# Joined 512-column matmuls of the high weights in chosen stages, an early first activation of TensorE, and 64x64 work put in groups

## The chip, the cores and the metric

The kernel runs on one core of one Trainium2 chip. What counts is the device time of one execution in microseconds (us). Before the change it is 2953.51 us, the median of 3 runs (2952.63 to 2953.68).

## The reference

The reference chains two transformer blocks over 256 tokens of width 1024 in float32; each block has two layers. What matters of them here:

```python
def swiglu(x, w_in, w_out):
    gate, up = jnp.split(x @ w_in, 2, axis=-1)
    return (jax.nn.silu(gate) * up) @ w_out

for l in range(2):                                   # first block
    h = h + 0.5 * swiglu(rms_norm(h, ffn1_norm[l]), ffn1_w_in[l], ffn1_w_out[l])
    u = rms_norm(h, mix_norm[l])
    ...                                              # u @ w_in[l]; state space branch y_s, delta rule branch y_d
    merged = sigmoid(gate_s) * (y_s @ ssm_w_branch[l]) + sigmoid(gate_d) * (y_d @ dn_w_branch[l])
    h = h + merged @ w_out[l]
    h = h + 0.5 * swiglu(rms_norm(h, ffn2_norm[l]), ffn2_w_in[l], ffn2_w_out[l])
for l in range(2):                                   # second block
    h = h + mixer_sublayer(...)                      # retention and a wide convolution, ends with @ w_mix_out
    h = h + memory_cross_attention(...)
    h = h + conv_ffn(...)                            # ends with @ w_down
```

A feed forward is 1024 to 2x2816 and 2816 back to 1024. There are four of the first block's kind (`ffn`) and two of the second's (`conv_ffn`). The delta rule needs the inverse of small triangular matrices, which the kernel makes by doubling blocks of 2 up to 64.

## The kernel before

**Numbers in two parts.** TensorE multiplies in a float32 form with a shorter mantissa (F32R). To keep precision, each operand is split into a rounded high part and a low rest. A product is three matmuls: high weights by high input, high weights by low input, low weights by high input.

**Weights.** `wpart` (L180 to L190) loads 128x1024 weights (one output tile, eight input tiles) on SyncE's DMA queue into `wr`, lets ScalarE round them into `wh` (L187), and VectorE subtract to get `wl` (L189). Each pool has four buffers, and `wpart` runs at high priority, so weights are made as far ahead as the buffers go.

**Inputs.** Activations are feature-major: a tile of 128x512 holds two feature tiles (256 tokens each). Class `X` keeps a list of high tiles and one of low tiles, each 512 wide; `h(k)` and `l(k)` cut 256 columns out of one.

**The product.** `proj_fm` (L201) makes two output tiles (m = 0, 1) of 256 columns side by side in one PSUM bank (`pw`, four of them). For each input tile k it issues three matmuls of 256 columns (L213, L214, L215), each with its own weight load. `proj_tm2` (L235) has the roles swapped: x is stationary, and the weights move in 512 columns (L246 to L248).

**The feed forward.** `ffn` (L350) runs 11 rounds j; in each a gate and an up product, `pg` and `pu`, are multiplied by `rbb` (1/rms of each token) on the way out of PSUM, since the input isn't normalised yet when the products begin; then silu, product, and the split into `hid`. `Norm.finish` gives `rb` some us after the stage has begun. `out_proj` (L345) multiplies by the second weights in four steps, each evicted by one VectorE instruction onto h (L368), which then feeds the next norm. `Norm.scaled` (L285) makes an input that is normalised, so that later products need no `rbb`; before, only the mixers use it.

**The delta rule.** `delta` (L497) is a generator that is advanced between projections (`tick`). Near its end, a loop over eight blocks alternates a 64x64 transpose (L621) and a 64x64 matmul (L622); then eight 64x64 matmuls follow (L630). It runs twice in each of the first block's layers.

**The order.** A planner simulates the program and writes the order of each engine's instructions from priorities; within an engine it is then fixed.

Of the kernel before, what the change touches and what calls it, by code (L numbers as in the profile page):

```python
# [15 lines left out]
P = 128  # L16
# [8 lines left out]
AHEAD = 100000  # L25
PUMP = 3.1
# [47 lines left out]
def _kernel(tc, t):  # L74
    nc = tc.nc
    V, A, G, TE = nc.vector, nc.scalar, nc.gpsimd, nc.tensor
    with ExitStack() as es:
# [5 lines left out]
        hp, xp = pool("hp", 4), pool("xp", 4)  # L83
# [16 lines left out]

        def pw():
            return pwp.tile([P, 512], F32, name="pw")
# [5 lines left out]
        g0 = cp.tile([P, 8], F32, name="g0")  # L108
        with tc.high_priority(offset=AHEAD):
            nc.sync.dma_start(g0, t["v1"][:, OFF1["ffn1_norm"][0]:OFF1["ffn1_norm"][0] + 8])  # L110
# [43 lines left out]
        def split(hi, lo, src):  # L154
            A.copy(hi, src)
            sub(lo, src, hi.bitcast(F32))
# [35 lines left out]
        class X:  # L192
            def __init__(self):
                self.hi, self.lo = [], []

            def h(self, k):
                return self.hi[k // 2][:, (k % 2) * 256:(k % 2) * 256 + 256]

            def l(self, k):
                return self.lo[k // 2][:, (k % 2) * 256:(k % 2) * 256 + 256]  # L200

        def proj_fm(w, i, KT, x):

            p = pw()
            for m in range(2):
                o = p[:, m * 256:m * 256 + 256]
                for k0 in range(0, KT, 8):
                    kt = min(8, KT - k0)
                    hi, lo = wpart(w[i + m, :, k0 * 128:(k0 + kt) * 128], kt * 128)
                    for kk in range(kt):  # L210
                        k = k0 + kk
                        a, b = hi[:, kk * 128:kk * 128 + 128], lo[:, kk * 128:kk * 128 + 128]
                        TE.matmul(o, a, x.h(k), start=(k == 0), stop=False)  # L213
                        TE.matmul(o, a, x.l(k), start=False, stop=False)  # L214
                        TE.matmul(o, b, x.h(k), start=False, stop=(k == KT - 1))  # L215
                    tick()
            return p

# [36 lines left out]
        class Norm:  # L255
            def __init__(self, g, alloc=None):
                self.g, self.x, self.acc = g, X(), None
                self.alloc = alloc
# [5 lines left out]
            def operand(self, j, h):  # L264
                if self.alloc is None:
                    hi = xp.tile([P, 512], F32R, name="xh")
                    lo = xp.tile([P, 512], F32R, name="xl")
                else:
                    hi, lo = self.alloc(F32R), self.alloc(F32R)
                for m in range(2):  # L270
                    k = 2 * j + m
                    s = slice(m * 256, m * 256 + 256)
                    A.activation(hi[:, s], h[:, s], AF.Copy, scale=self.g[:, k:k + 1])
                    V.scalar_tensor_tensor(lo[:, s], h[:, s], self.g[:, k:k + 1], hi[:, s].bitcast(F32), op0=ALU.mult, op1=ALU.subtract)
                self.x.hi.append(hi)
                self.x.lo.append(lo)
# [8 lines left out]
            def scaled(self, h):  # L285

                y = X()
                for j in range(4):
# [4 lines left out]
                    hi, lo = xp.tile([P, 512], F32R, name="xh"), xp.tile([P, 512], F32R, name="xl")  # L293
                    split(hi, lo, v)
                    y.hi.append(hi)
                    y.lo.append(lo)
# [48 lines left out]
        def out_proj(w, KT, x, evac):  # L345
            for j in range(4):
                evac(j, proj_fm(w, 2 * j, KT, x))


        def ffn(h, L, nrm, w1, w2, nxt):  # L350
# [3 lines left out]
            for j in range(NF // 2):  # L354
                pg = proj_fm(w1[L], 2 * j, 8, x)
                pu = proj_fm(w1[L], NF + 2 * j, 8, x)
                g, u = cv(), cv()
                mul(r2(g), r2(pg), rbb)
                A.activation(g, g, AF.Silu)
                mul(r2(u), r2(pu), rbb)  # L360
                mul(g, g, u)
                hi, lo = sa(F32R), sa(F32R)
                split(hi, lo, g)
                hid.hi.append(hi)
                hid.lo.append(lo)

            def evac(j, p):
                V.scalar_tensor_tensor(h[j], p, 0.5, h[j], op0=ALU.mult, op1=ALU.add)  # L368
                nxt.feed(j, h[j])
            out_proj(w2[L], NF, hid, evac)  # L370
# [32 lines left out]
        def to_features(tm, u, g, dst):  # L403
# [5 lines left out]
            hi, lo = sa(F32R), sa(F32R)  # L409
            n = 512 // g.shape[1]  # L410
            for m in range(g.shape[1]):
                s = slice(m * n, m * n + n)
                A.activation(hi[:, s], p[:, s], AF.Copy, scale=g[:, m:m + 1])
                V.scalar_tensor_tensor(lo[:, s], p[:, s], g[:, m:m + 1], hi[:, s].bitcast(F32), op0=ALU.mult, op1=ALU.subtract)
            dst.hi.append(hi)
            dst.lo.append(lo)

        def mixer1(h, L, nrm, nxt):
# [97 lines left out]
            def delta(hh, kf, qf, vf, zd):  # L516
# [296 lines left out]
            def evac_s(j, p):  # L813
                V.scalar_tensor_tensor(gs[j], gs[j], 1.0, p, op0=ALU.add, op1=ALU.mult)
                add(gs[j], gs[j], gd[j])
                hi, lo = sa(F32R), sa(F32R)
                split(hi, lo, gs[j])
# [517 lines left out]
```

## Time and profile before

| what | value |
|---|---|
| runs, median (lowest to highest) | 2953.51 us (2952.63 to 2953.68) |
| profiled execution, its own time | 2955.59 us |
| its span, first to last instruction | 2953.8 us |
| matmuls, and as many weight loads | 24912 |
| busy: TensorE, VectorE, ScalarE | 99%, 75%, 51% |

The span is what the rows tell of; 1.8 us of the profiled execution lie around it. In the rows PE is TensorE's matmul side, PEld its weight loads, DVE VectorE, ACT ScalarE, SPq the instruction queue of SyncE. A matmul's duration in the rows is from entry to exit of a pipeline, so durations overlap: the pace is read from start to start, or from the number in a stretch.

### The profile page before, as it was taken

To read this page: it belongs to the slowest core of one execution; us is meant where nothing else is said; L and a number is where in the kernel's file an instruction comes from. 1 tells how busy PE (TensorE), PEld (TensorE's weight loads), DVE (VectorE), ACT (ScalarE), POOL (GpSimd) and SP (SyncE) were. 2 spreads that over 40 slices of the span, in tenths; PEclk is the share of its full clock that TensorE was granted. 3 is DMA by queue.
4 is the path that set the end of the run, shared out by engine and by line. 5 is a ranking of instruction groups with operands and counts; after the bars stand their busy time and mean duration, and the time that the engine had idled before them with its cause. 6 is when DMAs were issued, how large, how long until landed. Compare 5 with 4: busy or idle time off the path is not lost.

```text
span 2953.8 us, 59625 instructions
## 1 busy us (share of the span) xinstructions
PE 2936.0 (99%) x24912; PEld 2840.5 (96%) x24912; DVE 2202.1 (75%) x3498; ACT 1516.1 (51%) x2016; POOL 98.7 (3%) x113
## 2 busy tenths in 40 slices
PE   8999999999999999999999999999999999999998
PEld 8999998999999999999999988999999988999998
DVE  6658878866566589688666799976676899876774
ACT  5446555554444465465444544545554544554553
POOL 0000001100000000011000000000000000000000
PEclk9999999999999999999999999999999999999999
DMA  6555444456565555344556555555456555554554
GB/s 230 178 183 173 151 137 142 156 182 185 178 186 180 182 175 163 126 147 150 179 182 195 170 188 167 172 175 168 157 181 194 185 173 167 172 179 150 174 181 132
DMA packets 141679, 505.34 MB, mean 171 GB/s; under 512 B 16164, under 2 KB 16550, under 8 KB 141408
## 3 DMA queue, kind: packets, MB, share of 16 engines
q1 hardware_dynamic: 137808, 490.29, 52.2%
q0 software_dynamic: 3312, 10.70, 1.3%
q8 instruction: 195, 3.19, 0.4%
q14 instruction: 76, 0.62, 0.1%
q10 hardware_dynamic: 288, 0.52, 0.0%
HBM read 500.32 MB, written 1.13 MB: 170 GB/s over the span
## 4 chain that ended last, share of the span: by engine, by line
PE 99%; DMA 0%; DVE 0%; issue 0%; ACT 0%; SPq 0%; POOLq 0%; DVEq 0%
PE pw L213 26%; PE pw L215 26%; PE pw L214 26%; PE pw L246 3%; PE pw L248 3%; PE pw L247 3%; PE pm L764 1%; PE pm L408 1%; PE pw L229 1%; PE pw L231 1%; PE pw L230 1%; PE pm L585 0%; PE pm L1080 0%; PE pm L1106 0%; PE pm L599 0%; PE pm L983 0%
## 5 line engine op out<-in xcount | busy, mean ns | idle before, releaser
L187 ACT CAST wh<-wr 128x1024 fp32r<-128x1024 f32 (+1 forms) x938 | 970.4, 1036 | 1223.9 <-PE pw L214 879.2
L189 DVE TENSOR_TENSOR wl<-wr,wh 128x1024 fp32r<-128x1024 f32 (+1 forms) x938 | 1130.2, 1207 | 521.1 <-ACT wh L187 512.0
L213 PE MATMUL pw<-xh,wh 128*128 128x256 f32 x3712 | 1066.3, 288 | 7.8 <-ACT wh L187 7.7
L214 PE MATMUL pw<-xl,wh 128*128 128x256 f32 x3712 | 1058.7, 285 | 0.0
L215 PE MATMUL pw<-xh,wl 128*128 128x256 f32 x3712 | 1056.4, 285 | 0.7 <-DVE wl L189 0.7
L214 PE MATMUL pw<-sa,wh 128*128 128x256 f32 x2656 | 752.7, 284 | 0.0
L213 PE MATMUL pw<-sa,wh 128*128 128x256 f32 x2656 | 751.8, 284 | 0.7 <-DVE sa L137 0.7
L215 PE MATMUL pw<-sa,wl 128*128 128x256 f32 x2656 | 751.6, 283 | 0.0
L213 PEld LDWEIGHTS pw<-xh,wh 128*128 128x128 f32 x3712 | 716.5, 193 | 13.3 <-ACT wh L187 10.0
L214 PEld LDWEIGHTS pw<-xl,wh 128*128 128x128 f32 x3712 | 717.2, 193 | 5.4 <-issue 4.6
L215 PEld LDWEIGHTS pw<-xh,wl 128*128 128x128 f32 x3712 | 716.7, 193 | 2.7 <-DVE wl L189 1.3
L214 PEld LDWEIGHTS pw<-sa,wh 128*128 128x128 f32 x2656 | 509.7, 192 | 0.9 <-issue 0.5
L213 PEld LDWEIGHTS pw<-sa,wh 128*128 128x128 f32 x2656 | 509.1, 192 | 1.3 <-issue 0.9
L215 PEld LDWEIGHTS pw<-sa,wl 128*128 128x128 f32 x2656 | 509.6, 192 | 0.8 <-issue 0.5
L925 DVE SCALAR_TENSOR_TENSOR sb<-sa,dw,sb 128x255 f32<-128x255 f32 (+26 forms) x480 | 201.2, 460 | 0.0
L246 PE MATMUL pw<-wh,xh 128*128 128x512 f32 x416 | 165.7, 398 | 0.0
L247 PE MATMUL pw<-wh,xl 128*128 128x512 f32 x416 | 163.4, 393 | 0.0
L248 PE MATMUL pw<-wl,xh 128*128 128x512 f32 x416 | 163.3, 396 | 0.0
L137 DVE TENSOR_TENSOR cv<-pw,rb 128x512 f32<-128x512 f32 x118 | 81.2, 691 | 64.5 <-PE pw L215 62.5
L386 DVE SCALAR_TENSOR_TENSOR cv<-pw,v,cv 128x255 f32<-128x255 f32 (+2 forms) x240 | 104.0, 471 | 0.2
L248 PEld LDWEIGHTS pw<-wl,xh 128*128 128x128 f32 x416 | 78.0, 189 | 17.1 <-issue 0.5
L246 PEld LDWEIGHTS pw<-wh,xh 128*128 128x128 f32 x416 | 78.7, 189 | 15.4 <-issue 0.5
(316 smaller groups left out, 2426.0 us busy)
## 6 DMA issues: line engine op xcount, KB each, us to landing
wr<-in_w1f_dram SPq DMA_DIRECT2D x128, 512.0 KB, 3.7
wr<-in_w2f_dram SPq DMA_DIRECT2D x96, 512.0 KB, 3.6
wr<-in_f1i_dram SPq DMA_DIRECT2D x88, 512.0 KB, 3.6
wr<-in_f2i_dram SPq DMA_DIRECT2D x88, 512.0 KB, 3.6
wr<-in_wup_dram SPq DMA_DIRECT2D x88, 512.0 KB, 3.6
wr<-in_w2t_dram SPq DMA_DIRECT2D x64, 512.0 KB, 4.0
wr<-in_w1t_dram SPq DMA_DIRECT2D x48, 512.0 KB, 3.9
wr<-in_f1o_dram SPq DMA_DIRECT2D x32, 512.0 KB, 3.5
```

Of the source, the lines that this page charges most:

```text
L137: V.tensor_tensor(out, a, b, op=ALU.mult)
L187: A.copy(hi[:, :n], r[:, :n])
L189: last[0] = V.tensor_tensor(lo[:, :n], r[:, :n], hi[:, :n].bitcast(F32), op=ALU.subtract)
L213: TE.matmul(o, a, x.h(k), start=(k == 0), stop=False)
L214: TE.matmul(o, a, x.l(k), start=False, stop=False)
L215: TE.matmul(o, b, x.h(k), start=False, stop=(k == KT - 1))
L229: TE.matmul(o, x.h(k)[:, s], a, start=(k == 0), stop=False)
L246: TE.matmul(p[tk], x.h(k)[:, s], a, start=(k == 0), stop=False)
L247: TE.matmul(p[tk], x.l(k)[:, s], a, start=False, stop=False)
L248: TE.matmul(p[tk], x.h(k)[:, s], b, start=False, stop=(k == 7))
L386: V.scalar_tensor_tensor(om[:, tap:], xm[:, :256 - tap], wc, om[:, tap:], op0=ALU.mult, op1=ALU.add)
L925: V.scalar_tensor_tensor(om[:, tap:], xm[:, :256 - tap], wc, om[:, tap:], op0=ALU.mult, op1=ALU.add)
```

## The change

- `X` keeps one tile of 128x512 for each input tile k: 256 columns high, then 256 columns low.
- `proj_fm` has a second form, used when an `evict` function is passed: one matmul of 512 columns applies the high weights to high and low input at once, and one of 256 columns applies the low weights. An output tile then takes a whole bank; the second half is added to the first at the end, by `into` (a ScalarE copy and a VectorE addition) or `onto` (two VectorE instructions onto h).
- The joined form is used in `ffn` from round 2 on (`EARLY = 2`), in all of its output products, in three of four steps of the state space output (`ssw`), in the last product of the second block's mixer (`wmo`), and in `conv_ffn`'s output (`wdn`). It is not used in `conv_ffn`'s first product, in `wo1`, in `wxo` and in the other projections.
- In `ffn`, `nrm.scaled(h, sa)` makes a normalised input in round 0, which rounds 2 to 10 use without `rbb`.
- At the beginning, a tile of ones is set, ScalarE copies one column, and three float32 matmuls of 512 columns run on it; the tiles of x are issued on ScalarE's DMA queue instead of SyncE's.
- In `delta`, the eight 64x64 transposes are issued first, then the eight 64x64 matmuls.

```diff
-        hp, xp = pool("hp", 4), pool("xp", 4)
+        hp, xp = pool("hp", 4), pool("xp", 8)
...
+        with tc.high_priority(offset=2 * AHEAD):
+            one = st()
+            V.memset(one, 1.0)
+            A.activation(one[:, 0:1], one[:, 0:1], AF.Copy)
+            warm = pw()
+            for _ in range(WARM):
+                TE.matmul(warm, one[:, :128], one, start=True, stop=True)
+            nc.scalar.dma_start(h[0], t["x"][0])
+            nc.sync.dma_start(g0, t["v1"][:, OFF1["ffn1_norm"][0]:OFF1["ffn1_norm"][0] + 8])
+            nc.scalar.dma_start(h[1], t["x"][1])
...
-        h = []
-        for j in range(4):
-            h.append(hp.tile([P, 512], F32, name="h"))
-            with tc.high_priority(offset=AHEAD - (0, 80, 80, 110)[j]):
-                nc.sync.dma_start(h[j], t["x"][j])
+            nc.scalar.dma_start(h[2], t["x"][2])
+            nc.scalar.dma_start(h[3], t["x"][3])
...
+            def add(self, src):
+                for m in range(src.shape[1] // 256):
+                    s = src[:, m * 256:m * 256 + 256]
+                    hi, lo = self.new()
+                    A.copy(hi, s)
+                    sub(lo, s, hi.bitcast(F32))
...
+                        if evict is not None:
+                            if k:
+                                TE.matmul(o[:, :256], b, x.h(k), start=False, stop=False)
+                            TE.matmul(o, a, x.t[k], start=(k == 0), stop=(k == KT - 1))
+                            if k == 0:
+                                TE.matmul(o[:, :256], b, x.h(k), start=False, stop=False)
...
+        def into(dst):
+            def evict(m, a, b):
+                s = dst[:, m * 256:m * 256 + 256]
+                A.copy(s, b)
+                add(s, a, s)
+            return evict
...
+                else:
+                    proj_fm(w1[L], 2 * j, 8, x, into(g))
+                    A.activation(g, g, AF.Silu)
+                    proj_fm(w1[L], NF + 2 * j, 8, x, into(u))
+                if j == EARLY - 2:
+                    xs = nrm.scaled(h, sa)
+                if j == EARLY - 1:
+                    x = xs
...
                     TE.transpose(pz[:64, o], y64[:64, o], ident[:64, :64])
+                for i in range(8):
+                    o = slice(i * 64, i * 64 + 64)
                     TE.matmul(pa[:64, o], M[i // 4][64:, (i % 4) * 128:(i % 4) * 128 + 64], y64[64:, o], start=True, stop=True)
```

## Rows read from the trace of the kernel before

**Rows 1.** The page's part 1: busy us, share of the span, instructions.

```profile
PE 2936.0 (99%) x24912; PEld 2840.5 (96%) x24912; DVE 2202.1 (75%) x3498; ACT 1516.1 (51%) x2016; POOL 98.7 (3%) x113
```

**Rows 2.** The page's part 4: the chain that ended last, by engine.

```profile
PE 99%; DMA 0%; DVE 0%; issue 0%; ACT 0%; SPq 0%; POOLq 0%; DVEq 0%
```

**Rows 3.** Stretches: length, busy (count) of PE PEld DVE ACT POOL, clock, DMA.

```profile
10.00:15.00 5.00, 4.63 (x20) 4.18 (x20) 4.94 (x9) 5.00 (x11) 0.00 (x0) 1.00 1.04 408
365.20:368.60 3.40, 3.40 (x41) 3.34 (x34) 3.37 (x10) 0.00 (x0) 0.00 (x0) 0.52 0.33 116
658.00:672.00 14.00, 14.00 (x119) 14.00 (x118) 10.33 (x13) 8.89 (x11) 0.00 (x0) 1.00 0.71 217
663.00:762.00 99.00, 99.00 (x827) 99.00 (x826) 64.28 (x69) 45.43 (x51) 0.00 (x0) 1.00 0.60 184
1797.00:1814.00 17.00, 17.00 (x77) 14.06 (x76) 16.53 (x34) 9.00 (x11) 2.04 (x2) 1.00 0.40 129
```

**Rows 4.** Timeline of PE: start us, length us, instruction; both sizes side by side.

```profile
206.71 0.40 PE L247 MATMUL pw<-wh,sa 128*128 128x512 f32 x1
206.94 0.28 PE L213 MATMUL pw<-sa,wh 128*128 128x256 f32 x1
207.06 0.62 PE L248 MATMUL pw<-wl,sa 128*128 128x512 f32 x2
207.51 0.39 PE L246 MATMUL pw<-wh,sa 128*128 128x512 f32 x1
```

**Rows 5.** Groups of instructions on PE: busy us, mean ns, idle before.

```profile
L213 PE MATMUL pw<-xh,wh 128*128 128x256 f32 x3712 | 1066.3, 288 | 7.8 <-ACT wh L187 7.7
L246 PE MATMUL pw<-wh,xh 128*128 128x512 f32 x416 | 165.7, 398 | 0.0
L959 PE MATMUL pm<-sa 128*128 128x512 f32 x16 | 8.2, 592 | 0.0
```

**Rows 6.** Timeline of PE at the 64x64 work.

```profile
361.23 0.24 PE L621 MATMUL pm<-ident,sa 64*64 64x64 f32 x1
...
364.65 0.57 PE L585 MATMUL pm<-st,sa 32*32 32x32 f32 x39
...
372.73 1.14 PE L630 MATMUL pm<-st 64*64 64x64 f32 x16
373.80 1.09 PE L643 MATMUL pm<-ident,sa 128*128 128x128 f32 x8
374.83 0.36 PE L599 MATMUL pm<-st 32*32 32x32 f32 x20
```

**Rows 7.** Timeline of ACT and PE at the beginning.

```profile
3.97 1.28 ACT L273 ACT_TABLE_LOAD   x1 [3.97 <-DMA h<-in_x_dram]
7.68 0.58 PE L213 MATMUL pw<-xh,wh 128*128 128x256 f32 x1 [7.68 <-ACT wh L187]
11.91 0.41 PE L213 MATMUL pw<-xh,wh 128*128 128x256 f32 x1
16.82 0.31 PE L215 MATMUL pw<-xh,wl 128*128 128x256 f32 x1
```

**Rows 8.** Groups of instructions on DVE and ACT: busy us, mean ns.

```profile
L189 DVE TENSOR_TENSOR wl<-wr,wh 128x1024 fp32r<-128x1024 f32 x888 | 1083.1, 1221 | 453.7 <-ACT wh L187 444.6 <-PE pm L647 4.0 <-PE pw L230 0.7
L137 DVE TENSOR_TENSOR cv<-pw,rb 128x512 f32<-128x512 f32 x118 | 81.2, 691 | 64.5 <-PE pw L215 62.5 <-ACT rb L331 1.6
L292 DVE SCALAR_TENSOR_TENSOR st<-h,v,rb 128x256 f32<-128x256 f32 x24 | 10.1, 475 | 0.0
L143 DVE TENSOR_TENSOR st<-st,pm 128x256 f32<-128x256 f32 x16 | 6.6, 413 | 5.0 <-PE pm L599 5.0
L331 ACT COPY rb<-pm 128x256 f32<-128x256 f32 x14 | 5.2, 371 | 14.0 <-PE pm L329 14.0
```

**Rows 9.** Timeline of PE and DVE at the second feed forward's beginning.

```profile
645.91 0.28 PE L213 MATMUL pw<-xh,wh 128*128 128x256 f32 x1
...
658.57 0.69 DVE L137 TENSOR_TENSOR cv<-pw,rb 128x512 f32<-128x512 f32 x1 [0.24 <-ACT rb L331]
```

More of the change, by code (lines that the diff above doesn't have):

```diff
@@ L25 @@
 AHEAD = 100000
+EARLY = 2
+WARM = 3
 PUMP = 3.1
@@ L99, in cv, with xt @@
             return vp.tile([P, 512], F32, name="cv")
+        def xt(dt=F32):
+            return xp.tile([P, 512], dt, name="xt")
         def pw():
@@ L264, in operand @@
             def operand(self, j, h):
[L265 to L276, printed above, removed]
+                self.x.add_scaled(h, self.g[:, 2 * j:2 * j + 2])
             def square(self, h):
@@ L283, in finish, with scaled @@
                 return self.x, self.rs, self.rb
-            def scaled(self, h):
-                y = X()
+            def scaled(self, h, alloc=xt):
+                y = X(alloc)
                 for j in range(4):
@@ L292, in scaled @@
                         V.scalar_tensor_tensor(v[:, s], h[j][:, s], self.g[:, 2 * j + m:2 * j + m + 1], self.rb, op0=ALU.mult, op1=ALU.mult)
[L293 to L296, printed above, removed]
+                    y.add(v)
                 return y
@@ L343, in stats, with out_proj, out_residual @@
             return rs, rows(rs, name)
-        def out_proj(w, KT, x, evac):
+        def out_proj(w, KT, x, evac, wide=0):
             for j in range(4):
-                evac(j, proj_fm(w, 2 * j, KT, x))
+                if j < wide:
+                    y = st()
+                    proj_fm(w, 2 * j, KT, x, into(y))
+                else:
+                    y = proj_fm(w, 2 * j, KT, x)
+                evac(j, y)
+        def out_residual(w, KT, x, h, scale, nxt, wide=True):
+            for j in range(4):
+                if wide:
+                    proj_fm(w, 2 * j, KT, x, onto(h[j], scale))
+                else:
+                    p = proj_fm(w, 2 * j, KT, x)
+                    if scale == 1.0:
+                        add(h[j], p, h[j])
+                    else:
+                        V.scalar_tensor_tensor(h[j], p, scale, h[j], op0=ALU.mult, op1=ALU.add)
+                nxt.feed(j, h[j])
         def ffn(h, L, nrm, w1, w2, nxt):
@@ L408, in to_features @@
                     TE.transpose(p[:, m * 256 + c * 128:m * 256 + c * 128 + 128], tm[c][:, (2 * u + m) * 128:(2 * u + m) * 128 + 128], ident)
[L409 to L416, printed above, removed]
+            dst.add_scaled(p, g)
         def mixer1(h, L, nrm, nxt):
@@ L1031, in mixer2 @@
             mem.values(range(1))
-            def evac(j, p):
-                V.scalar_tensor_tensor(h[j], p, 0.5, h[j], op0=ALU.mult, op1=ALU.add)
-                nxt.feed(j, h[j])
-            out_proj(t["wmo"][L], 8, mg, evac)
+            out_residual(t["wmo"][L], 8, mg, h, 0.5, nxt)
         class Memory:
@@ L1118, in xattn @@
             drain()
-            def evac(j, p):
-                add(h[j], p, h[j])
-                nxt.feed(j, h[j])
-            out_proj(t["wxo"][L], 8, xo, evac)
+            out_residual(t["wxo"][L], 8, xo, h, 1.0, nxt, False)
         def conv_ffn(h, L, nrm, nxt):
@@ L1136, in conv_ffn @@
                 mul(o, o, u)
-                hi, lo = sa(F32R), sa(F32R)
-                split(hi, lo, o)
-                hid.hi.append(hi)
-                hid.lo.append(lo)
-            def evac(j, p):
-                add(h[j], p, h[j])
-                nxt.feed(j, h[j])
-            out_proj(t["wdn"][L], NF, hid, evac)
+                hid.add(o)
+            out_residual(t["wdn"][L], NF, hid, h, 1.0, nxt)
         class Final:
```

108 lines of the change are left out of this document (54 added, 54 removed).

## The prediction

> **What bounds the kernel now.** I read the page's busy shares first: TensorE is busy 99% of the span, VectorE 75%, ScalarE 51% [rows 1]. Since a matmul's duration overlaps the next one's, a busy TensorE could still be waiting, so the chain that ended last comes next: 99% of it is TensorE [rows 2]. So nothing but fewer or cheaper instructions of TensorE makes the kernel faster, and the other engines matter only where they would make it wait.
>
> The pace is then read from stretches without other work. In 99 us of a feed forward's first product 827 matmuls of 256 columns ran; some two were already under way when the stretch opened, so one takes 99/825 = 0.120 us. In 17 us of a stretch of 512-column matmuls there are 77, so 17/75 = 0.227 us [rows 3]. In both, each matmul has a weight load of its own. 256 more columns cost 0.107 us, and what is left of either, 13 ns, is paid once per matmul whatever its width. The durations say the same from another side: 398 against 288 ns, 110 ns for 256 columns [rows 5]. The sizes also add up when they alternate: a 512-column matmul at 206.71 is followed 0.23 us later by one of 256, and that one 0.12 us later by the next of 512 [rows 4].
>
> **The join.** Before, an output tile and an input tile cost three matmuls, 0.360 us. Joined, they are one of 512 and one of 256, 0.227 + 0.120 = 0.347 us: 13 ns less. How many: a feed forward's first product has 9 joined rounds x 2 products x 2 output tiles x 8 = 288, its second 8 x 22 = 176; four of them make 1856. The state space output has 6 x 16 = 96 in each of two layers, `wmo` 8 x 8 = 64 twice, `wdn` 8 x 22 = 176 twice: 672 more. Together 2528 pairs, as many matmuls and weight loads fewer, and 2528 x 13 ns = **32.9 us**. The bounds: the one at 206.71 takes 0.23 us [rows 4], which with rounding can be 0.233, and then a pair saves 7 ns, 17.7 us; the two merged behind it take 0.225 us each (207.06 to 207.51), and a pair saves 15 ns, 38 us. I take 13 ns, from the longest clean stretch. A pair that cost more than 0.360 us would need a 512-column matmul over 0.240 us, which no row of a clean stretch has.
>
> The Trainium skill, "TensorE: Matmul & The Clock Gate", section "Back-to-back issue gap", puts the isolated gap at columns/2.4 GHz plus 2.5 ns. By that fixed part the join would save 2528 x 2.5 = 6 us and not 33, and the sum below would be 27 us higher; the rows here have 13 ns, and I go by them.
>
> **What the join asks of the other engines.** A joined output tile is evicted by an ACT copy of 256 columns and a DVE addition: 0.37 and 0.41 us, where half of a 0.69 us multiplication stood [rows 8]. For a round j of the first product, DVE has four `wl` (4.88), four additions (1.65), the product (0.69) and two subtractions (0.83): 8.1 us. TensorE needs 32 x 0.347 = 11.1 us for it. So this is hidden, by 3 us of room per round, and ACT's load is lighter still. The second product has 15.3 us per step against some 10.4 of DVE. `wmo` is the one place where it doesn't fit: 16 x 0.347 = 5.55 us of TensorE, against two `wl` (2.44), four additions onto h (1.90), two operands (0.95) and the sum of squares (0.68), 6.0 us. Over four steps DVE ends 1.7 us late; four buffers of weights made ahead cover some of it. It happens twice: 0 to 3.4 us, I take **1**.
>
> **The normalised input.** This is the piece that may cost. `scaled` is new in each of the four `ffn`: eight multiplications of 0.475 us and eight subtractions of 0.41, 7.1 us of DVE [rows 8], and eight more copies on ACT. It can't begin before `rb`, whose first user runs at 658.57. The first matmul of this feed forward is at 645.91 [rows 9]; two rounds of 96 matmuls later, at 645.91 + 192 x 0.12 + 0.7 for the statistics' own matmuls, 669.7, round 2 wants the first of the eight tiles, and the last 2.5 us later. In 658 to 672 DVE is busy 10.3 of 14 us already [rows 3]; with 7.1 more it has 17.4. So it is 3.4 us late if nothing gives way. What can give way are the `wl` (four ahead is 11 us of TensorE) and round 1's products. What is late next is TensorE itself: round 2's first matmul, and every one behind it, since its order is fixed. Between 0 and 3.4 us per feed forward, I take 1.5, near the middle as it depends on the planner's order: 4 x 1.5 = **6 us** lost, bounds 0 and 14.
>
> **The 64x64 work.** A site runs from 361.23 to 364.65, 3.42 us for eight transposes and eight matmuls in alternation. Eight 64x64 matmuls on end take 372.73 to 373.80, 1.07 us; eight transposes on end, of twice the size, 1.03 us [rows 6]. Grouped, a site should take 1.07 plus 0.5 to 1.03, so it saves 1.3 to 1.85 us. There are four sites: 5.3 to 7.4 us, and I take **6.9**, near the upper end since the transposes are smaller than those of the row. The copies behind them wait for the last instruction as before.
>
> **The beginning.** The first x tile lands, a table load of 1.28 us follows on ACT, then its operand, then the first weights, and TensorE starts at 7.68. It runs at half pace (0.213 us a matmul: from 11.91 to 16.82 there are 23) and from 16.82 on at 0.12 [rows 7]; half pace is that of the 1.2 GHz level, though the clock column of rows 3 has 1.00 for 10 to 15 us; I go by the starts. The rise came 9 us after the first matmul, 5 after the starts had become regular. The change moves the table load ahead of x (1.28 us) and gives TensorE work before. Three float32 matmuls of 512 columns are some 3 us at full pace (16 records of 8 instructions, 8.2 us [rows 5]), 6 at half. If the clock is up when x comes, 23 x 0.093 = 2.1 us are won besides. At most: 34 matmuls, 4.1 us of work, were done by 16.82; started at 6.4 without a gap they end at 10.5, a gain of 6.3. At least: DMA is full at 408 GB/s in 10 to 15 us [rows 3], and if the data are the limit only about 1 us is won. I take **4**. The Trainium skill, "Trainium Kernel Development and Optimization", section "Key Constraints", says that DMAs of all queues run on the same 16 engines and that several issuers save issue time alone; by it the move of x to ACT's queue gives nothing beyond its order. The full DMA share in the row agrees.
>
> **Clock drops.** In 365.2 to 368.6 the granted clock is 0.52, the 1.2 GHz level [rows 3], right behind a 64x64 site; such a drop costs up to half its 3.4 us, 1.7. Less thin work ahead of it may remove it: 0 to 6.8 us if each of the four sites has one, I take **2**.
>
> **Sum.** -32.9 - 6.9 - 4 - 2 + 6 + 1 = -38.8 us. On the span of 2953.8 that is 2915.0; the profiled execution's own 2955.59 becomes 2916.8. The median of the runs is 2953.51, 2.1 below that execution, so the prediction for the median is **2915 us**.
>
> **Rivals.** (a) The join pays half, 7 ns a pair: 2930 us. For it: in rows 4 the 512s stand 0.23 us apart; against it: the longer stretch. Chance 0.17. (b) With the weights held and x moving, a 512-column matmul costs as much as two of 256, 0.240 us, because the 13 ns go with the columns there: the join gives nothing, and the sum is -6.9 - 4 - 2 + 7 = -5.9, 2948 us. Against it: no row has a clean 0.240, and the roles differ only in which operand is loaded. Chance 0.05, half of it within 0.2%. The Trainium skill's fixed part, in the section named above, lies near this one, with 2941. (c) DVE at the four openings and at `wmo` is late in full, 14 + 3.4 us: 2926 us. For it: 17.4 us of work in 14. Chance 0.10. (d) The planner puts the work elsewhere, so the grouped blocks are spread by other work and the first matmuls come no earlier: -32.9 + 7, 2928 us. Chance 0.05. (e) Slower: a joined output tile holds a bank alone, so the four `pw` banks hold four output tiles and not eight, and an eviction needs ACT, then DVE, each behind its queue. TensorE has three banks, 8.3 us, before it stalls. It decides if each of the 36 joined rounds takes 1.2 us more than 11.1, since the gains come to some 44 us; that needs 12.3 us of a chain where I count 8.1 of DVE. At 1.5 us a round it is 2964 us. Chance 0.08, a third of it within 0.2%. My forecast has the remaining 0.55, with its own range of 2903 to 2924.
>
> **How the numbers follow.** A measurement can tell 0.2%, 5.9 us. Faster by more are the forecast, (a), (c), (d) and half of (b): 0.895, so 0.90. No change: the other half of (b) and a third of (e), 0.05. Slower: the rest of (e), 0.05. The range takes in (a), (c) and (d) and leaves out (b), (e) and what beats most bounds at once: 2901 to 2938.
>
> **What the profile after would show.** 22384 matmuls and weight loads, plus the six records of the first three. In a feed forward's second product 0.347 us a pair, so 61 us where 63 stand for 528 matmuls. A 64x64 site of 1.6 to 2.1 us. The first matmuls on weights at 0.12 us. The first joined matmul of each `ffn` with an idle gap of 0 to 3.4 us ahead, released by DVE's subtraction. The prediction is wrong if the 512-column matmul with weights held still runs slower than 0.233 us, or if TensorE shows gaps behind evictions within the rounds.

## The result, and the profile after

The changed kernel takes 2916.99 us, the median of 4 runs (2916.69 to 2917.46); the kernel before took 2953.6 beside it (2952.63 to 2954.8). The ratio is 0.9876, 95% interval 0.9859 to 0.9893. The forecast was 2915, so the total is 2 us off. Its terms are not that good: the join gave 24 us and not 33, and three smaller terms made up for it. Of the experiments below, one run of `e7_high_first` took 5955.69 us, twice the time of all others, and is left out of its numbers.

Line numbers have moved: `proj_fm` has L251 and L254 (low weights, 256 columns) and L252 (high weights, 512 columns) in the joined form, L256 to L258 in the old one; `wh` is L197, `wl` L199, the product L150, the addition L153, the subtraction L156, `scaled` L342.

The page after: part 1 and, from part 4, the chain that ended last by engine.

```profile
span 2915.0 us, 55446 instructions
...
PE 2900.8 (100%) x22390; PEld 2691.3 (92%) x22390; DVE 2268.5 (78%) x3865; ACT 1577.2 (54%) x2327; POOL 103.6 (4%) x113
...
PE 39%; DVE 0%; POOLq 0%; DVEq 0%; issue 0%; ACT 0%
```

The 2522 records fewer than in [rows 1] are the 2528 joined matmuls, less the six of the warm beginning. DVE and ACT have 3 points more work, spread over many more instructions. The chain's shares add up to only 39% in this page, so it proves less than [rows 2]; what it holds is TensorE. More telling is the list of TensorE's waits after the beginning: in 1620 to 1980 us it holds one,

```profile
PE pw L308 <- ACT st L1022: 1.6, 1, 1.6
```

and the kernel before had one of 0.7 us there. That is a loss of 1 us in the second block's first mixer, which no term of the forecast had; no experiment was spent on it, and its cause is not shown.

TensorE's order of projections is the same in both kernels, so the two traces can be cut at the same matmuls. The table has stage lengths in us from the first matmul of a stage to the first of the next one.

| stage | before | after | difference | how often |
|---|---|---|---|---|
| first feed forward, rounds 0 and 1, with the beginning | 36.8 | 33.9 | -2.9 | 1 |
| rounds 0 and 1 of the other `ffn` | 23.9 | 23.9 | 0.0 | 3 |
| `ffn`, rounds 2 to 10 | 103.7 | 100.65 | -3.0 | 4 |
| `ffn`, second product | 63.35 | 61.85 | -1.5 | 4 |
| first block's mixer, with the delta rule | 342.2, 342.9 | 335.2, 337.0 | -7.0, -5.9 | 2 |
| state space output | 47.05 | 46.0 | -1.05 | 2 |
| `wmo` | 23.0 | 22.4 | -0.6 | 2 |
| `wdn` | 63.4 | 62.1 | -1.2 | 2 |
| second block's mixers, to `wmo` | 347.9, 346.1 | 348.9, 346.1 | +1.0, 0.0 | 2 |
| all others | | | 0 | |

The joined stages give 4 x 3.0 + 4 x 1.5 + 2 x (1.05 + 0.6 + 1.2) = 23.7 us, 9.4 ns for each of the 2528 pairs. The delta rule's stages give 12.9, the beginning 2.9, and the openings of `ffn` cost nothing.

**The pace of a pair.** Stretches of the kernel before, rounds 2 to 10 and the second product of the second `ffn`:

```profile
669.90:773.60 103.70, 103.70 (x866) 103.70 (x866) 67.13 (x72) 47.95 (x54) 0.00 (x0) 1.00 0.59 181
773.60:837.00 63.40, 63.40 (x530) 63.40 (x529) 34.98 (x38) 28.31 (x35) 0.00 (x0) 1.00 0.60 186
```

The same two stretches after, and `wdn`:

```profile
654.50:755.10 100.60, 100.60 (x578) 87.67 (x576) 70.23 (x103) 57.68 (x99) 0.00 (x0) 1.00 0.61 191
755.10:817.00 61.90, 61.90 (x355) 53.94 (x354) 38.90 (x51) 28.93 (x38) 0.00 (x0) 1.00 0.64 191
2204.30:2266.40 62.10, 62.10 (x354) 53.97 (x353) 39.17 (x51) 28.69 (x36) 0.00 (x0) 1.00 0.65 197
```

TensorE is busy throughout, at clock 1.00, so nothing waits: the pairs themselves are slower than 0.347 us. 100.6/288 is 0.349, 61.9/176 is 0.352, 62.1/176 is 0.353. The starts show two paces. TensorE's timeline after, within one output tile of the first `ffn`, and within one of `wdn`:

```profile
79.14 0.40 PE L252 MATMUL pw<-sa,wh 128*128 128x512 f32 x1
79.37 0.28 PE L251 MATMUL pw<-sa,wl 128*128 128x256 f32 x1
...
81.22 0.62 PE L252 MATMUL pw<-sa,wh 128*128 128x512 f32 x2
...
2214.75 0.40 PE L252 MATMUL pw<-sa,wh 128*128 128x512 f32 x1
2214.99 0.28 PE L251 MATMUL pw<-sa,wl 128*128 128x256 f32 x1
...
2217.23 0.40 PE L252 MATMUL pw<-sa,wh 128*128 128x512 f32 x1
```

From 79.14 to 81.22 are six pairs, 0.347 each: the additive pace of [rows 4]. From 2214.75 to 2217.23 are seven, 0.354 each. A whole output tile has the one pace or the other. In rounds 2 to 10 they alternate tile by tile, after a few mixed ones; in a second product all output tiles from the fourth on have 0.353; in `wdn` all eight have. The durations (397 and 280 ns in the groups below against 398 and 288 in [rows 5]) don't show this at all.

```profile
L252 PE MATMUL pw<-sa,wh 128*128 128x512 f32 x2528 | 871.5, 397 | 0.0
L251 PE MATMUL pw<-sa,wl 128*128 128x256 f32 x2308 | 643.2, 280 | 0.0
```

**The opening of the second `ffn`,** in answer to [rows 9]: DVE's timeline, and then PE's at round 2's first matmul.

```profile
642.95 1.29 DVE L150 TENSOR_TENSOR cv<-pw,rb 128x512 f32<-128x512 f32 x2 [0.25 <-ACT rb L378]
644.16 3.25 DVE L342 SCALAR_TENSOR_TENSOR st<-h,v,rb 128x256 f32<-128x256 f32 x8
647.32 1.22 DVE L199 TENSOR_TENSOR wl<-wr,wh 128x1024 fp32r<-128x1024 f32 x1
...
650.86 1.76 DVE L156 TENSOR_TENSOR sa<-st,sa 128x256 fp32r<-128x256 f32 x5
652.54 0.68 DVE L150 TENSOR_TENSOR cv<-pw,rb 128x512 f32<-128x512 f32 x1
653.14 0.42 DVE L156 TENSOR_TENSOR sa<-st,sa 128x256 fp32r<-128x256 f32 x1
```

```profile
654.11 0.28 PE L258 MATMUL pw<-xt,wl 128*128 128x256 f32 x1
654.23 0.40 PE L252 MATMUL pw<-sa,wh 128*128 128x512 f32 x1
```

In the kernel before, DVE had 3.2 us free in the same stretch, from its first use of `rb` to round 2:

```profile
658.57:669.84 11.27, 11.27 (x96) 11.27 (x95) 8.07 (x9) 6.92 (x8) 0.00 (x0) 1.00 0.69 224
```

Now it has no gap worth the name between 642.95 and 654.23 (11.28 us busy in 11.28), yet the last of the eight subtractions ends at 653.56, 0.67 us before round 2, and that round reads the eighth tile only some 2.4 us later. Eight multiplications take 3.25 us and not 8 x 0.475, and five subtractions 1.76: durations of DVE overlap as well, and start to start it is 0.40 and 0.34 us. So `scaled` costs 8 x (0.40 + 0.34) = 5.9 us where the forecast had 7.1, and the products and `wl` of [rows 3] shrink in the same way. One `wl` fewer stands in this stretch than before (three, not four), and round 0's own subtraction has moved behind round 2's first matmul; TensorE doesn't wait for either.

**The 64x64 site,** in answer to [rows 6]: PE's timeline.

```profile
351.81 0.63 PE L682 MATMUL pm<-ident,sa 64*64 64x64 f32 x8
352.37 1.14 PE L685 MATMUL pm<-sa 64*64 64x64 f32 x16
353.44 0.75 PE L646 MATMUL pm<-st,sa 32*32 32x32 f32 x64
```

A site takes 1.63 us instead of 3.42; four of them give 7.2. The rest of the 12.9 goes with the clock. This stretch after has the 1.2 GHz level, as 365.20 in [rows 3] had:

```profile
433.60:437.00 3.40, 3.40 (x13) 2.82 (x12) 3.32 (x11) 1.47 (x3) 1.14 (x1) 0.53 0.44 153
```

Before, low clock in the delta rule's stages adds up to seven stretches of 3.4 us, after to three; four fewer at up to 1.7 us are up to 6.8, and 12.9 - 7.2 = 5.7 was won.

**The beginning,** in answer to [rows 7]: ACT and then PE.

```profile
1.18 1.28 ACT L119 ACT_TABLE_LOAD   x1 [1.18 <-PEq L1360]
```

```profile
2.73 5.02 PE L122 MATMUL pw<-st 128*128 128x512 f32 x6 [2.73 <-ACT st L119]
7.18 0.68 PE L256 MATMUL pw<-xt,wh 128*128 128x256 f32 x1
7.70 0.28 PE L257 MATMUL pw<-xt,wh 128*128 128x256 f32 x1
7.82 0.29 PE L258 MATMUL pw<-xt,wl 128*128 128x256 f32 x1
...
10.28 0.39 PE L257 MATMUL pw<-xt,wh 128*128 128x256 f32 x1 [0.63 <-DVE xt L232]
...
12.41 0.39 PE L258 MATMUL pw<-xt,wl 128*128 128x256 f32 x1 [0.43 <-DVE wl L199]
```

From 7.70 on the starts are 0.12 us apart, where the kernel before went at half pace until 16.82. But now TensorE waits for the next input tile and for low weights. Both waits end with VectorE, and VectorE has no idle time there:

```profile
10.00:15.00 5.00, 4.05 (x29) 3.66 (x30) 5.00 (x9) 3.48 (x7) 0.00 (x0) 1.00 1.03 403
```

### The profile page after: what moved, and what is told of

It is laid out like the page before. It is cut to its first block, busy times and chain, and to the rows that moved or that the text cites. A ratio compares the mean times of both kernels' runs of the same rounds, so it can differ in the third digit from the quotient of the medians.

```text
span 2915.0 us, 55446 instructions
## 1 busy us (share of the span) xinstructions
PE 2900.8 (100%) x22390; PEld 2691.3 (92%) x22390; DVE 2268.5 (78%) x3865; ACT 1577.2 (54%) x2327; POOL 103.6 (4%) x113
## 5 line engine op out<-in xcount | busy, mean ns | idle before, releaser
L197 ACT CAST wh<-wr 128x1024 fp32r<-128x1024 f32 (+1 forms) x938 | 969.9, 1037 | 1148.5 <-PE pw L257 447.0
L199 DVE TENSOR_TENSOR wl<-wr,wh 128x1024 fp32r<-128x1024 f32 (+1 forms) x938 | 1131.6, 1209 | 483.4 <-ACT wh L197 475.7
L252 PE MATMUL pw<-sa,wh 128*128 128x512 f32 x2528 | 871.5, 397 | 0.0
L256 PE MATMUL pw<-xt,wh 128*128 128x256 f32 x2560 | 736.4, 288 | 0.3 <-ACT wh L197 0.2
L258 PE MATMUL pw<-xt,wl 128*128 128x256 f32 x2560 | 727.1, 284 | 0.4 <-DVE wl L199 0.4
L257 PE MATMUL pw<-xt,wh 128*128 128x256 f32 x2560 | 726.4, 284 | 0.6 <-DVE xt L232 0.6
L251 PE MATMUL pw<-sa,wl 128*128 128x256 f32 x2308 | 643.2, 280 | 0.0
L252 PEld LDWEIGHTS pw<-sa,wh 128*128 128x128 f32 x2528 | 458.6, 188 | 94.0
L256 PEld LDWEIGHTS pw<-xt,wh 128*128 128x128 f32 x2560 | 490.6, 192 | 7.0 <-issue 2.6
L257 PEld LDWEIGHTS pw<-xt,wh 128*128 128x128 f32 x2560 | 491.0, 192 | 6.4 <-issue 4.3
L258 PEld LDWEIGHTS pw<-xt,wl 128*128 128x128 f32 x2560 | 490.9, 192 | 1.7 <-issue 0.7
L251 PEld LDWEIGHTS pw<-sa,wl 128*128 128x128 f32 x2308 | 435.0, 189 | 11.0
L257 PE MATMUL pw<-sa,wh 128*128 128x256 f32 x1280 | 362.7, 284 | 0.0
L258 PE MATMUL pw<-sa,wl 128*128 128x256 f32 x1280 | 361.5, 283 | 0.0
L256 PE MATMUL pw<-sa,wh 128*128 128x256 f32 x1280 | 361.4, 284 | 0.0
L258 PEld LDWEIGHTS pw<-sa,wl 128*128 128x128 f32 x1280 | 245.2, 192 | 0.8 <-issue 0.5
L256 PEld LDWEIGHTS pw<-sa,wh 128*128 128x128 f32 x1280 | 244.8, 192 | 0.6
L979 DVE SCALAR_TENSOR_TENSOR sb<-sa,dw,sb 128x243 f32<-128x243 f32 (+27 forms) x480 | 202.8, 466 | 0.0
L308 PE MATMUL pw<-wh,xt 128*128 128x512 f32 x416 | 167.2, 402 | 1.6 <-ACT st L1022 1.6
L309 PE MATMUL pw<-wh,xt 128*128 128x512 f32 x416 | 164.3, 395 | 0.0
```

The lines of the kernel that those rows point to most:

```text
L197: A.copy(hi[:, :n], r[:, :n])
L199: last[0] = V.tensor_tensor(lo[:, :n], r[:, :n], hi[:, :n].bitcast(F32), op=ALU.subtract)
L251: TE.matmul(o[:, :256], b, x.h(k), start=False, stop=False)
L252: TE.matmul(o, a, x.t[k], start=(k == 0), stop=(k == KT - 1))
L308: TE.matmul(p[tk], x.h(k)[:, s], a, start=(k == 0), stop=False)
L309: TE.matmul(p[tk], x.l(k)[:, s], a, start=False, stop=False)
```

## The experiments

**All joins off** (`e1_no_join`). Warm beginning and grouping stay.

```diff
-EARLY = 2
+EARLY = 99
...
-        def out_residual(w, KT, x, h, scale, nxt, wide=True):
+        def out_residual(w, KT, x, h, scale, nxt, wide=False):
...
-            out_proj(t["ssw"][L], 16, ys, evac_s, 3)
+            out_proj(t["ssw"][L], 16, ys, evac_s, 0)
```

> All joined matmuls are undone, and with them the early normalised input of the four feed forwards; the warm beginning and the grouped 64x64 work stay. Theory 1, from the two traces by stage: the joined stages are 23.9 us shorter (9.5 ns a pair) and the openings cost nothing, so this kernel should take 2917 + 24 = 2941 us. Rival, the prediction's sum: the join gives 32.9 us and some 7 us are lost at the openings and evictions, so 2917 + 26 = 2943 us in all, but then the joined stages alone should be 33 us longer and the stages of the first two rounds 6 us shorter than in the changed kernel.

Measured: 2940.63 us (2940.27 to 2941.21), ratio to before 0.9955 (0.994 to 0.997). Every joined stage is longer again by its difference in the table, and rounds 0 and 1 of the later `ffn` stay at 23.9. So the join is worth 23.6 us and its openings cost nothing.

**The 64x64 work alternating again** (`e2_alternate`).

```diff
                     TE.transpose(pz[:64, o], y64[:64, o], ident[:64, :64])
-                for i in range(8):
-                    o = slice(i * 64, i * 64 + 64)
                     TE.matmul(pa[:64, o], M[i // 4][64:, ...], y64[64:, o], start=True, stop=True)
```

> The changed kernel with transposes and matmuls of 64x64 in alternation again. Theory 1: the grouping gives its instructions' own time, 7.4 us, and also spares the clock drops that stood behind the sites, so that drops come back in the first block's mixers and the kernel takes 12 to 13 us more, 2929 to 2930 us. Rival: the instructions alone, 7.4 us, 2924 us, and the number of clock drops stays at three, because where they fall was chance.

Measured: 2928.46 us (2928.15 to 2930.26), ratio 0.9915 (0.9899 to 0.9932): 11.5 us lost, 6.4 and 4.9 of the span in the two delta rule stages, nothing elsewhere. The groups are back at the durations of before (245 and 242 ns, in the changed kernel 221 and 219), and six stretches of low clock stand where the changed kernel has three:

```profile
447.30:450.70 3.40, 3.40 (x18) 3.40 (x18) 0.84 (x3) 1.51 (x2) 0.00 (x0) 0.52 0.42 142
```

Three stretches at up to 1.7 and four sites at 1.8 make up to 12.3, so theory 1 holds and the rival's 2924 us falls.

**No warm matmuls** (`e3_no_warm`): `WARM = 0`. The table load stays early and x on ACT's queue.

> The changed kernel without the three float32 matmuls on ones; the early table load and the x tiles on the other queue stay. Theory 1: TensorE then does its first matmuls at half pace until some 5 to 9 us after the first, and 1 to 3 us are lost, 2918 to 2920 us. Rival: the beginning is bound by the weights and inputs as they arrive and are split, TensorE waits for them at either pace, and the time is the same within 0.5 us; or better by up to 1 us, since the first matmul on weights at 7.2 us stood behind the last of the three.

Measured: 2915.93 us (2914.69 to 2917.69), ratio 0.9871 (0.9857 to 0.9886), no difference from the changed kernel that can be told. The trace says why: the beginning is 1.8 us longer,

```profile
6.09 0.58 PE L255 MATMUL pw<-xt,wh 128*128 128x256 f32 x1 [6.09 <-ACT wh L196]
6.47 0.41 PE L256 MATMUL pw<-xt,wh 128*128 128x256 f32 x1
...
8.15 0.41 PE L257 MATMUL pw<-xt,wl 128*128 128x256 f32 x1
8.37 0.41 PE L255 MATMUL pw<-xt,wh 128*128 128x256 f32 x1
```

at half pace from 6.09 to 16.4, and in the second delta rule stage the profiled execution had no low stretch where the changed kernel's had two, 3.3 us. By these two traces the matmuls are worth 1.8 of the beginning's 2.9; the other 1.1 belong to the earlier table load, to x and to whatever else the change moves there (not parted). That is not clear of the scatter: in the traces of the ten kernels with the warm matmuls this stage takes 33.9 to 34.4 us eight times, 35.2 in `e4_by_two` and 36.6 in `e10_phase`. The warm matmuls also hold the first real one back by a microsecond: 7.18 against 6.09.

**More joins** (`e6_more_joins`): `wo1`, `wxo` and, from round 2, `conv_ffn`'s first product.

```diff
-                pg = proj_fm(t["wup"][L], NF + 2 * j, 8, x)
-                pv = proj_fm(t["wup"][L], 2 * j, 8, x)
...
+                else:
+                    g = cv()
+                    proj_fm(t["wup"][L], NF + 2 * j, 8, x, into(g))
+                    conv_silu(g, None, w, 3, NF, 2 * j, bias, o)
+                    proj_fm(t["wup"][L], 2 * j, 8, x, into(u))
+                if j == EARLY - 2:
+                    xs = nrm.scaled(h, sa)
```

> The changed kernel with joined matmuls also in the first product of conv_ffn from round 2 on (with an early normalised input there too) and in wo1 and wxo. Theory 1: the other engines have room there too, 576 pairs gain 10.5 ns as in the feed forwards and 256 gain 9 ns, 8 us in all, 2909 us. Rival: VectorE, which has the convolution there besides, some 10 us of work in a round of 11.1 and 6 more at the opening, comes late, TensorE waits for it, and the time is 2915 us or more.

Measured: 2920.29 us (2917.33 to 2923.73), ratio 0.9887 (0.9871 to 0.9904). `wo1` gives 0.6 us each time, `wxo` 0.1, but `conv_ffn`'s first product takes 131.8 us instead of 127.6. It is the opening; PE's timeline, and the stretch behind it:

```profile
2097.10 0.28 PE L258 MATMUL pw<-xt,wl 128*128 128x256 f32 x1
2101.45 0.77 PE L252 MATMUL pw<-sa,wh 128*128 128x512 f32 x1 [4.07 <-DVE sa L156]
```

```profile
2102.00:2108.80 6.80, 6.80 (x27) 5.92 (x26) 5.90 (x14) 1.34 (x3) 0.00 (x0) 0.61 0.41 138
```

Here DVE has the convolution besides, and the stall of rival (c) is real: 4.1 us waiting for a subtraction, and behind the idle time TensorE goes at the 1.2 GHz level for some 6 us. So the rival holds: the same construction that costs nothing in `ffn` costs more here than its join saves.

**Low weights over 512 columns too** (`e5_low512`). The low weights are applied to the low input as well, a term that the kernel leaves out, so every joined matmul has 512 columns.

```diff
-                                TE.matmul(o[:, :256], b, x.h(k), start=False, stop=False)
+                                TE.matmul(o, b, x.t[k], start=False, stop=False)
```

> The low weights too are applied to high and low input at once, so a pair is two matmuls of 512 columns (it adds the product of the two low parts, which the reference's tolerance doesn't need, and leaves nothing out). Theory 1: a 512-column matmul with held weights costs 227 ns, as in the stretch of the kernel before, and what makes a pair 350.5 ns is the mixture of sizes; a pair is then 454 ns, and the kernel 2528 x 103.5 ns = 262 us longer, 3179 us. Rival: held weights cost 234 ns at 512 columns whatever stands beside, a pair is 468 ns, and the kernel takes 3214 us.

Measured: 3172.42 us in a single run. Rounds 2 to 10 take 130.6 us for 288 pairs, a second product 79.8 for 176: 0.453 in both. So a 512-column matmul with weights held costs 0.2265 us, the price of [rows 3], and the missing microseconds belong to the mixture of two widths, not to the wide matmul.

**The order within pairs** (`e4_by_two`: 256, 256, 512, 512 everywhere; `e8_outputs_by_two`: that in the output products alone; `e7_high_first`: strict alternation from 512 on, without the turn that the changed kernel makes at the beginning of each output tile).

```diff
 e7_high_first
-                            if k:
-                                TE.matmul(o[:, :256], b, x.h(k), start=False, stop=False)
-                            TE.matmul(o, a, x.t[k], start=(k == 0), stop=(k == KT - 1))
-                            if k == 0:
-                                TE.matmul(o[:, :256], b, x.h(k), start=False, stop=False)
+                            TE.matmul(o, a, x.t[k], start=(k == 0), stop=False)
+                            TE.matmul(o[:, :256], b, x.h(k), start=False, stop=(k == KT - 1))
```

> The changed kernel with the joined matmuls ordered by twos: two of 256 columns, then two of 512. Theory 1: a pair takes 350.5 ns instead of 347 because sizes alternate; by twos it comes closer to 347, and the kernel gains up to 2528 x 3.5 ns = 9 us, 2908 us. Rival: a 512-column matmul with held weights takes 231 to 241 ns whatever stands next to it, and the time stays at 2917 us within 2 us.

> The changed kernel with the order by twos only in the output products (feed forwards, conv_ffn, wmo, state space output), where it made the stages 0.3 to 1.1 us shorter, and the old order in the feed forwards' first products, where it made them 0.3 us longer. From those stages: 4 x 0.8 + 2 x (0.4 + 0.3 + 1.1) = 6.8 us shorter than the changed kernel, 2910 us. Rival: the gain of the order by twos is within the scatter of the beginning and of the clock drops, and the time stays at 2914 to 2917 us.

> The changed kernel with strict alternation, the joined matmul first for every input tile, so that no two of one size meet at an output tile's end or beginning. In the changed kernel's trace whole output tiles take either 346.7 or 353.6 to 354.5 ns a pair, and the pace changes only where an output tile ends. Theory 1: the doubled sizes at those places switch the pace; without them one pace holds throughout a stage, and the feed forwards' first products (100.6 us in the changed kernel, half their tiles at each pace) become either 99.7 or 101.9 us: the kernel is then at 2913 or at 2922 us or a mixture by stage, but no longer alternates by tile. Rival: something else sets the pace (the bank or the weight buffer in use), and tiles still alternate, 2917 us.

| | median us | ratio (95%) | rounds 2 to 10 | second product | state space output | `wmo` | `wdn` |
|---|---|---|---|---|---|---|---|
| changed kernel | 2916.99 | 0.9876 (0.9859 to 0.9893) | 100.65 | 61.85 | 46.0 | 22.4 | 62.1 |
| `e4_by_two` | 2912.88 | 0.9862 (0.9848 to 0.9877) | 100.95 | 61.3 | 45.85 | 22.4 | 61.3 |
| `e8_outputs_by_two` | 2910.49 | 0.9854 (0.9839 to 0.9869) | 100.65 | 61.3 | 45.85 | 22.4 | 61.3 |
| `e7_high_first` (three runs) | 2907.92 | 0.985 (0.9834 to 0.9867) | 99.9 | 61.0 | 46.0 | 22.6 | 62.2 |

By twos a pair takes 0.348 us in the long output tiles (second products and `wdn`) and 0.351 in the short ones of rounds 2 to 10, so `e4_by_two` gained in part only. The stages of `e8_outputs_by_two` give 4.0 us where 6.8 were expected. With the strict alternation every output tile of rounds 2 to 10 from the fourth on, and of `ffn`'s second product, goes at 0.347, so theory 1 of `e7_high_first` holds there and its rival falls (in the first three tiles the planner's order still repeats a width):

```profile
78.13 0.39 PE L250 MATMUL pw<-sa,wh 128*128 128x512 f32 x1
78.36 0.28 PE L251 MATMUL pw<-sa,wl 128*128 128x256 f32 x1
...
80.90 0.39 PE L250 MATMUL pw<-sa,wh 128*128 128x512 f32 x1
```

Eight pairs in 2.77 us, over an output tile's boundary. But `wdn`, with the same sequence unbroken, keeps 0.353 in all eight output tiles. The medians of `e7` and `e8` also have luck in them: their profiled executions had one stretch of low clock against three, worth some 3 us; the stage columns are free of that.

**Is the pace a state?** (`e10_phase`). As `e7_high_first`, but in second products each step's second output tile begins with a group of 2, 3, 4 or 5 matmuls of 512 and then as many of 256.

```diff
+                            g = first[m] if k0 == 0 else 1
+                            if 0 < kk < g:
+                                continue
+                            ks = range(g) if kk == 0 else (kk,)
+                            for q in ks:
+                                TE.matmul(o, hi[:, q * 128:q * 128 + 128], x.t[k0 + q], start=(k0 + q == 0), stop=False)
+                            for q in ks:
+                                TE.matmul(o[:, :256], lo[:, q * 128:q * 128 + 128], x.h(k0 + q), start=False, stop=(k0 + q == KT - 1))
```

> The strict alternation as before, but in the second product of every feed forward (22 input tiles to an output tile) the second output tile of each step begins with a group: 2, 3, 4 or 5 times 512 on end, then as often 256, by step; the first output tile of each step has no group. Theory 1 (the pace, 347 or 354 ns a pair, is a state that lasts while the alternation is unbroken): it changes only at the groups, holds through the output tile without one that follows, and both paces turn up in both kinds of feed forward; 2910 us give or take 4. Rival (the pace belongs to the stage: its data, its neighbours on other engines): the pairs behind the groups go on at 347 in the first block's feed forwards and at 354 in the second's, as without groups, and the time is the same or 1 us less for the grouped ones.

Measured: 2916.51 us in a single run, above what either theory expected: there are three stretches of low clock and a fourth in the beginning, which takes 2.6 us more than in `e7_high_first`, and the second products of `ffn` take 1.0 us more each. The pace behind the group, output tile by output tile (groups in the second, fourth, sixth and eighth), ns a pair:

| | 1 | 2 | 3 | 4 | 5 to 8 |
|---|---|---|---|---|---|
| each of the four `ffn` | 347 | 353 | 353 | 353 | 353 |
| each of the two `wdn` | 353 | 347 | 347 | 353 | 353 |

PE's timeline at the first group of a `wdn`:

```profile
2209.78 0.40 PE L256 MATMUL pw<-sa,wh 128*128 128x512 f32 x1
...
2211.90 0.64 PE L256 MATMUL pw<-sa,wh 128*128 128x512 f32 x2
2212.38 0.40 PE L258 MATMUL pw<-sa,wl 128*128 128x256 f32 x2
...
2221.97 0.39 PE L256 MATMUL pw<-sa,wh 128*128 128x512 f32 x1
...
2223.70 0.40 PE L256 MATMUL pw<-sa,wh 128*128 128x512 f32 x1
```

Six pairs ahead of the group take 2.12 us, 0.353 each; nine microseconds behind it five take 1.73, 0.346. In an `ffn` it goes otherwise:

```profile
764.67 0.63 PE L256 MATMUL pw<-sa,wh 128*128 128x512 f32 x2
...
765.38 0.40 PE L256 MATMUL pw<-sa,wh 128*128 128x512 f32 x1
...
766.42 0.62 PE L256 MATMUL pw<-sa,wh 128*128 128x512 f32 x2
...
771.70 0.40 PE L256 MATMUL pw<-sa,wh 128*128 128x512 f32 x1
...
773.82 0.40 PE L256 MATMUL pw<-sa,wh 128*128 128x512 f32 x1
```

Behind the group of two the next three pairs still take 1.04 us, 0.347 each; then the planner's order repeats a width once more, at 766.42, and from there on the pace is slow (771.70 to 773.82, six pairs in 2.12). `e7_high_first` has that second repetition alone and stays at 0.347. So the pace is not a property of the stage. In `wdn` the group of two turned it to fast and the group of three back; in `ffn` the group of two with the repetition behind it turned it to slow; the other groups turned nothing, and it held through the output tiles without a group. Theory 1 holds in that.

One regularity stands in the traces, though no run was made for it. At the slow pace the starts of the 512-column matmuls repeat after three pairs (`wdn` of the changed kernel: 0.35, 0.35 and 0.36 us apart). Where two of 512 and two of 256 follow on at least five slow pairs in the changed kernel's trace, the pace stays slow in all 36 places with 6, 15 or 21 pairs ahead, multiples of three, and turns fast in all 71 places with 7 or 8. An output tile of 22 input tiles leaves 21 pairs between two such places and one of 8 leaves 7, which fits `wdn` and rounds 2 to 10. For the turn from fast to slow no such count was found: behind seven fast pairs it came in 74 places and not in 3.

**Each stage in its shortest order** (`e9_best`): strict alternation in `ffn`, by twos in the state space output, `wmo` and `wdn`, and `wo1` joined, by twos as well; `conv_ffn`'s first product stays as it was.

```diff
+                            if kk % two:
+                                continue
+                            ks = range(kk, min(kk + two, kt))
...
-            out_residual(t["wo1"][L], 8, mg, h, 0.5, nxt, False)
+            out_residual(t["wo1"][L], 8, mg, h, 0.5, nxt)
```

> Each stage in the order that was shortest so far: 512, 256 in strict alternation in the feed forwards, two and two in the state space output, `wmo` and `wdn`, and the output product of the first block's mixer joined too (in the same two and two). Theory 1 (a pair costs by its order, and stages don't touch each other): against the changed kernel 0.75 less in each of four first products, 0.8 in each of four second ones, 0.4 twice in the state space output, 0.3 twice at wmo, 1.1 twice at wdn, 0.6 twice at the newly joined product: 11 us, 2906 us, with 3.4 us to either side for where the clock falls. Rival (the newly joined product delays the next feed forward's opening, as the conv feed forward's join did): the openings of the second and fourth feed forward wait 2 us or more each, 2910 us or over.

Measured: 2906.72 us (2904.51 to 2908.13, 5 runs), ratio 0.9839 (0.9825 to 0.9852), the shortest median, though its interval overlaps with that of `e7_high_first`. Against the changed kernel by stage: 0.75 less each in rounds 2 to 10, 0.85 in second products, 0.3 in the state space output, 0.1 at `wmo`, 0.8 at `wdn`, 0.7 at `wo1`. The opening behind `wo1` stays at 23.9, so the rival falls. These make 10.2; theory 1 had 11. The span of the profiled execution is 11.8 shorter; it has one stretch of low clock fewer, up to 1.7 us.

## Why the prediction came out as it did

- **What bounds the kernel.** Right. Nearly all that was won is TensorE's own time, and the one place where another engine was put in its way (`e6_more_joins`) lost at once.
- **The join** is the term that was mis-sized: -23.7 measured, -32.9 forecast, 9.4 ns a pair and not 13. The price of the wide matmul was right (`e5_low512`), and so was 0.347 for a pair, but only for a part of the output tiles. The step that failed is to let the sizes add up from one place in [rows 4]: one 512 and one 256 in that row are no proof of a pace over eight or 22 pairs. The forecast's own sign of being wrong, a 512-column matmul slower than 0.233 us, is there in the slow tiles: from its start to that of the next matmul it takes 0.237 us in the mean. Rival (a), at 7 ns, is what a slow output tile pays (0.360 - 0.353), so the truth lay between forecast and rival. Rival (b), 0.240 us for the wide matmul, falls with `e5_low512`. The Trainium skill's fixed part ("TensorE: Matmul & The Clock Gate", section "Back-to-back issue gap", 2.5 ns, given there for an isolated matmul and not for a stream of weight loads and matmuls) would, as an estimate, make the join worth 6 us. `e1_no_join` has 23.6, so the rows decide against it here.
- **The openings:** +6 forecast, 0 measured. One step took DVE's durations for its pace, though those of TensorE were said to overlap: start to start `scaled` takes 5.9 us and not 7.1, which is 1.2 of the 3.4 us of lateness. The rest is what the forecast had named as able to give way, one `wl` and a subtraction of round 0; the 1.5 us taken between 0 and 3.4 were too many. The place was right: DVE has no idle time there and is done 0.67 us before round 2, and where it had the convolution to do as well, the stall came and took 4.1 us, and 6 us of low clock behind it.
- **Evictions, `wmo`, banks:** +1 forecast, 0 measured; no wait of TensorE there, so rival (e) falls.
- **The 64x64 work:** -6.9 forecast, -7.2 measured at the four sites, and `e2_alternate` loses it again. The groups stayed together, so rival (d) falls.
- **Clock drops:** -2 forecast, some -5.7 measured, as what is left of the delta rule's stages beside the sites. The place was right, the number of stretches was not counted: seven in the trace before, where the forecast read one. How many stay is partly luck (three here, one to three in the other kernels with grouped sites).
- **The beginning:** -4 forecast, -2.9 measured, some 1.8 of it from warm matmuls (`e3_no_warm`, one trace of each). The pace rose where it should, then TensorE waited for input tiles and low weights. The forecast feared the DMA, full in [rows 3]; the waits end with VectorE, which is busy without a break, and the same row of the kernel before had VectorE at 4.94 and ScalarE at 5.00 of 5.00 us. With x on ACT's queue DMA moves 403 GB/s in that stretch, 408 before. The Trainium skill, "Trainium Kernel Development and Optimization", section "Key Constraints", says that DMAs of all queues run on the same 16 engines. The two rates agree with it, but the move of x alone was not tried.
- **Not foreseen:** +1.0 in a mixer whose matmuls the change leaves alone up to `wmo` (its inputs are split in halves, so ACT and DVE have more instructions), with one wait of 1.6 us for ACT. The cause was not tried.

Sum of what was measured: -23.7 - 7.2 - 5.7 - 2.9 + 1.0 = -38.5 (the spans differ by 38.8), nearly the sum forecast, by errors of +9.2 (join), -6 (openings), -1 (evictions), -3.7 (clock), -0.3 (64x64), +1.1 (beginning) and +1.0 (mixer) that cancel. That the total is right within 2 us is luck.

## What to carry to other kernels

Where one engine is busy throughout, cost a change by its pace start to start over a long stretch of exactly the sequence that will run; neither durations nor the sum of two separate paces is enough, and this holds for the engine that must keep up, too. Where two widths of matmul alternate, try both strict alternation and twos, stage by stage: here the order alone was worth 8.8 us by stage in `e9_best`, a quarter of the change. A joined form that needs its input normalised first is free only where VectorE has room at the opening; read that stretch before putting it there.

## What was not expected of the hardware

- Alternating matmuls of 512 and 256 columns run at either 0.347 or 0.353 us a pair, with no wait, at clock 1.00. The pace holds while the alternation is unbroken (in `e7_high_first` from the fourth output tile of rounds 2 to 10 on at the one pace, through 176 pairs of `wdn` at the other) and turns at some repetitions of a width: from slow to fast, in the changed kernel's trace, just where the number of pairs ahead is no multiple of three. What makes it so stays open.
- A 64x64 transpose and a 64x64 matmul in turn take 3.42 us for eight of each; in two groups 1.63.
- Kernels with the same delta rule and grouped sites had one to three stretches of low clock in it in their profiled executions, at different places, up to 1.7 us each; the two with alternating sites had seven and six. This is as much as some of the effects here, so stages were compared and not totals.
